# The opening of a hybrid decoder step: samples of x in one 128-row tile, the first x chunk in halves, first weights on another queue

## The chip, the cores and the metric

The kernel runs on one core of a Trainium2 chip. The metric is the device time of one execution in microseconds (us). Before the change, three runs gave a median of 1380.89 us (1379.9 to 1382.13). The engines are named as the profile names them: PE (TensorE; PEld is its weight load), DVE (VectorE), ACT (ScalarE), POOL (GpSimd) and SP (SyncE, which here only issues DMAs).

## The reference, cut to what matters

One layer of a decoder for 256 prompt tokens and 8 x 4 sample tokens, 288 rows of x with 2048 features: state-space heads and sliding-window attention side by side, a cross-attention to 256 memory tokens, a SwiGLU feed-forward, RMS norms before each. The change concerns only the first lines of it:

```
def rmsnorm(x, w):
    y = x * rsqrt(mean(x * x, axis=-1) + EPS)
    return y * w
h = rmsnorm(x, norm_mix)
proj = h @ w_in        # 2048 -> z, xbc, dt, q, k, v
```

The kernel multiplies x with `norm_mix` before the product and with the reciprocal root after it, so products can start before the mean of the squares is known.

## The kernel before, in words

All activations are kept transposed: features on the 128 partitions, the 288 rows of x (256 prompt, 32 sample) along the free axis. A product in full accuracy is three products of parts (`mm3`, L167 to L171): each operand is split into a rounded high part and the remainder, and the terms low x high, high x high and high x low are summed in PSUM. The three lines L169, L170 and L171 are nearly all of PE's work. Weights come by `wload` (L142): a DMA on SP's queue into a `raw` buffer (3 of them), a cast on ACT to `hi` (L159), a subtraction on DVE to `lo` (L79).

The opening (L339 to L362) runs over four chunks of 512 features of x. For a chunk, `load_x` (L273) brings three tiles by SP: 128 + 128 prompt rows and 32 sample rows, 512 features each. `split_x` (L280) transposes them in pieces of 128 features on PE (L118; three pieces for one k, four k in a chunk) into one PSUM tile for each k, ACT writes the high part times `norm_mix` (L85, tile `xa`), DVE the remainder (L82), and DVE copies the transposed x itself (L293). `square_x` (L296) sums squares on ACT. Into these steps go the products of the keys and values (256 columns of `w_in`, two weight tiles of two k in chunk 0) and those of the first queries (`q_chunk`, one 512 KB tile for a chunk, whose columns are permuted while they are cast). `NWARM` = 8 products on zeros stand twice as fillers, at L219 and L345; in plain f32 each call is two passes on PE.

The order of the instructions on each engine is fixed at build time by a planner: it takes the instructions that are ready in its own model of time, the earliest in the program first, unless `high_priority` moves a block ahead; the whole opening is moved ahead. `in_turn` (L120) keeps the marked instructions of an engine in program order among themselves. The planner also puts in the waits, by the regions of the tiles that instructions read and write. POOL's queue issues the loads of the small vectors at the start (L228 to L240), ACT's queue that of `norm_mix`. An `Exp` on an empty column at L212 makes ACT load its function table early.

Of the kernel before, what the change touches and what calls it, by code (L numbers as in the profile page):

```python
# [8 lines left out]
F32 = mybir.dt.float32  # L9
F32R = mybir.dt.float32r  # L10
I32 = mybir.dt.int32
AF = mybir.ActivationFunctionType
# [3 lines left out]
P = 128  # L16
D = 2048
KC = D // P
TP = 256
TS = 32  # L20
# [26 lines left out]
def tile_hymba_step(ctx: ExitStack, tc: tile.TileContext, I: dict, O: list, stop: int = 99):  # L47
# [4 lines left out]
    def tl(pool, shape, dt, tag):  # L52
        uid[0] += 1
        return pool.tile(shape, dt, name=f"{tag}_{uid[0]}", tag=tag)
# [27 lines left out]
        nc.vector.scalar_tensor_tensor(out=out, in0=in0, scalar=s, in1=in1, op0=op0, op1=op1)  # L82

    def act(out, in_, func, scale=1.0, bias=0.0, accum_out=None):
        nc.scalar.activation(out=out, in_=in_, func=func, scale=scale, bias=bias, accum_out=accum_out)  # L85

    def f32(ap):
        return ap.bitcast(F32)
# [26 lines left out]
    def transpose(out, in_):  # L115
        k = in_.shape[0]
        b = in_.base_partition() if callable(in_.base_partition) else in_.base_partition
        nc.tensor.transpose(out, in_, ident[b:b + k, 0:k])  # L118

    def in_turn(ins):  # L120
        tc.keep_in_program_order(ins)
# [17 lines left out]
            clock[0] = max(clock[0], pend[0][0])  # L139
            step(0)  # L140

    def wload(pieces, nk, nm, ahead=AHEAD, perm=False):  # L142
        raw = tl(p_raw, [P, 1024], F32, "raw")
        hi = tl(p_hi, [P, 1024], F32R, "hi")
        lo = tl(p_lo, [P, 1024], F32R, "lo")
        n = nk * nm
        rv, hv, lv = (t[:, :n].rearrange("p (k m) -> p k m", m=nm) for t in (raw, hi, lo))
        with tc.high_priority(offset=ahead):
            for sel, ap in pieces:
                nc.sync.dma_start(sel(rv), ap)  # L150
        with tc.high_priority(offset=min(ahead, SPLIT_AHEAD)):
            if perm:
                src = raw[:, :n].rearrange("p (k g m c) -> m p k g c", g=2, m=2, c=64)
                h_, l_ = (t[:, :n].rearrange("p (k m g c) -> m p k g c", g=2, m=2, c=64) for t in (hi, lo))
                parts = [(h_[m], l_[m], src[m]) for m in range(2)]
            else:
                parts = [(hi[:, :n], lo[:, :n], raw[:, :n])]
            for h_, l_, src in parts:
                nc.scalar.copy(h_, src)  # L159
# [120 lines left out]
    def split_x(cp, pcs):  # L280
        pss = []
        for k in range(4):
            kk = cp * 4 + k
            ps = psum()
            pss.append(ps)
# [5 lines left out]
        for k in range(4):  # L291
            st = tl(p_xb, [P, T], F32, "xb")
            nc.vector.tensor_copy(st, pss[k][:, :T])  # L293
            xst.append(st)

    def square_x(cp, pcs):  # L296
        for t3 in range(3):
            n = P if t3 < 2 else TS
            act(tm(n=n), pcs[t3][:n], AF.Square, accum_out=ssqx[:n, t3, cp:cp + 1])

    def x_rstd():
        rx = stat[:, 22:25]
# [22 lines left out]
    def tm(w=512, n=P, dt=F32):  # L325
        return tl(mxm, [P, 512], dt, "m")[:n, :w]
# [9 lines left out]
                 wq[:, k0:k0 + nk, O_Q + 512 * g + P * rp:O_Q + 512 * g + P * rp + P]) for g in range(2)], nk  # L336

    pkq = [acc() for _ in range(4)]
    xp_ = load_x(0)  # L339
    for cp in range(4):  # L340
        if cp == 0:
            kvw = [wload(wslice(w_in, 2 * i, 2, O_K, 256), 2, 256, 0) for i in range(2)]
            split_x(0, xp_)
            for _ in range(NWARM):
                nc.tensor.matmul(pkq[3][:, 0:P], wm, wm, start=True, stop=True)  # L345
            square_x(0, xp_)
        else:
            kvw = [wload(wslice(w_in, 4 * cp, 4, O_K, 256), 4, 256, 0)]
        qw = [wload(*q_chunk(0, 4 * cp), 256, ahead=0, perm=True)]
        if cp < 3:  # L350
            xp_ = load_x(cp + 1)
        if cp == 2:
            nc.sync.dma_start(cst[:, C_ONE:], I["cst"][:, C_ONE:])
        gemm_w(pkq[:2], kvw, 4 * cp, KC, xmix)
        if cp < 3:
            square_x(cp + 1, xp_)
            split_x(cp + 1, xp_)
            if cp == 2:
                x_rstd()
        else:  # L360
            x_rstd_rows()
        gemm_w(pkq[2:], qw, 4 * cp, KC, xmix)  # L362
# [1095 lines left out]
```

## Time and profile before

| | us |
|---|---|
| median of three runs | 1380.89 |
| profiled execution | 1382.05 |
| its span | 1380.3 |
| PE busy in the span | 1367.6 |
| DVE busy | 810.5 |
| ACT busy | 638.4 |
| POOL busy | 84.4 |

The span runs from the first to the last instruction of the profiled execution; the execution's own time has in addition what lies around it. PE's busy time counts pipelined matmuls, which overlap, so it says that something is always under way on PE, not that it runs at its peak. The chain of work goes back from the last instruction to what released it, step by step. The granted TensorE clock is at full speed through the whole span.

### The profile page before, as it was taken

The page shows a single profiled execution, that of the slowest core. Times are in us where ns is not written, and L with a number is a line of the kernel's source. Part 1 is how long each engine was busy: PE and PEld are TensorE (multiplying, and loading weights), DVE is VectorE, ACT ScalarE, POOL GpSimd, SP SyncE. Part 2 cuts the span into 40 slices and gives each one's busy share as a digit, 9 for nine tenths or more (in the row PEclk, how much of TensorE's full clock was granted, in tenths as well). Part 3 has the DMA queues.
Part 4 walks back from the last instruction along what each step waited for, and adds up shares of the span by engine and source line. Part 5 has one row for each costly group of instructions (what it writes and reads, how often), then busy time and mean ns, then how long its engine had stood idle before and what let it go on. Part 6 is the DMA issues. An engine that isn't in the chain of part 4 may idle for free.

```text
span 1380.3 us, 26140 instructions
## 1 busy us (share of the span) xinstructions
PE 1367.6 (99%) x10637; PEld 1334.1 (97%) x10637; DVE 810.5 (59%) x1444; ACT 638.4 (46%) x1042; POOL 84.4 (6%) x139
## 2 busy tenths in 40 slices
PE   9999999999999999999999999999999999999997
PEld 8999999999998999999999999999999999999997
DVE  6886798876565567545545444444544544545554
ACT  7456867644454556433333333333333433434332
POOL 2010100004210122000000000000000000000110
PEclk9999999999999999999999999999999999999999
DMA  9665476588558645555555555555555555555552
GB/s 255 187 195 141 127 229 199 145 246 222 168 168 272 207 149 169 168 168 166 164 164 165 168 163 163 165 167 171 165 168 168 167 169 165 164 158 166 167 169 92
DMA packets 251392, 241.17 MB, mean 175 GB/s; under 512 B 12778, under 2 KB 242576, under 8 KB 251272
## 3 DMA queue, kind: packets, MB, share of 16 engines
q1 hardware_dynamic: 248424, 234.79, 55.7%
q0 software_dynamic: 2816, 4.70, 1.4%
q8 instruction: 83, 1.36, 0.4%
q14 instruction: 37, 0.30, 0.1%
q10 hardware_dynamic: 32, 0.01, 0.0%
HBM read 227.59 MB, written 11.85 MB: 173 GB/s over the span
## 4 chain that ended last, share of the span: by engine, by line
PE 96%; DVE 2%; ACT 1%; issue 1%; DMA 0%; POOL 0%; DVEq 0%; ACTq 0%; POOLq 0%
PE mm L169 29%; PE mm L170 29%; PE mm L171 29%; PE ps L118 3%; DVE xa L82 1%; PE ps L823 0%; DVE lo L79 0%; PE ps L521 0%; DMA xT<-xspill 0%; PE ps L1162 0%; ACT hi L159 0%; PE ps L899 0%; PE ps L1197 0%; PE ps L912 0%; PE ps L1235 0%
## 5 line engine op out<-in xcount | busy, mean ns | idle before, releaser
L79 DVE TENSOR_TENSOR lo<-raw,hi 128x1024 fp32r<-128x1024 f32 (+1 forms) x413 | 478.1, 1160 | 449.4 <-ACT hi L159 444.4
L159 ACT CAST hi<-raw 128x1024 fp32r<-128x1024 f32 (+1 forms) x413 | 410.5, 997 | 542.1 <-PE mm L171 446.7
L169 PE MATMUL mm<-xa,lo 128*128 128x288 f32 x2016 | 599.8, 298 | 0.6 <-ACT xa L174 0.6
L170 PE MATMUL mm<-xa,hi 128*128 128x288 f32 x2016 | 597.0, 296 | 0.0
L171 PE MATMUL mm<-xa,hi 128*128 128x288 f32 x2016 | 590.3, 293 | 0.0
L169 PEld LDWEIGHTS mm<-xa,lo 128*128 128x128 f32 x2016 | 378.0, 187 | 4.8 <-issue 3.1
L171 PEld LDWEIGHTS mm<-xa,hi 128*128 128x128 f32 x2016 | 379.1, 188 | 1.0 <-issue 0.7
L170 PEld LDWEIGHTS mm<-xa,hi 128*128 128x128 f32 x2016 | 378.8, 188 | 0.9 <-issue 0.3
L169 PE MATMUL mm<-ls,lo 128*128 128x288 f32 x512 | 152.4, 298 | 0.0
L171 PE MATMUL mm<-ls,hi 128*128 128x288 f32 x512 | 151.6, 296 | 0.0
L170 PE MATMUL mm<-ls,hi 128*128 128x288 f32 x512 | 151.0, 295 | 0.0
L169 PE MATMUL mm<-xb,lo 128*128 128x288 f32 x448 | 132.2, 295 | 2.9 <-DVE xT L79 2.8
L170 PE MATMUL mm<-xb,hi 128*128 128x288 f32 x448 | 132.6, 296 | 0.0
L171 PE MATMUL mm<-xb,hi 128*128 128x288 f32 x448 | 131.9, 294 | 0.0
L79 POOL TENSOR_TENSOR ssum<-ssum,ls 128x288 f32<-128x288 f32 x43 | 47.5, 1104 | 881.4 <-ACT ls L85 880.5
L170 PEld LDWEIGHTS mm<-ls,hi 128*128 128x128 f32 x512 | 96.7, 189 | 0.1
L169 PEld LDWEIGHTS mm<-ls,lo 128*128 128x128 f32 x512 | 96.6, 189 | 0.1
L171 PEld LDWEIGHTS mm<-ls,hi 128*128 128x128 f32 x512 | 96.3, 188 | 0.0
L169 PEld LDWEIGHTS mm<-xb,lo 128*128 128x128 f32 x448 | 84.6, 189 | 3.6 <-DVE xT L79 3.4
L171 PEld LDWEIGHTS mm<-xb,hi 128*128 128x128 f32 x448 | 84.6, 189 | 0.2 <-DVE xb L79 0.2
L170 PEld LDWEIGHTS mm<-xb,hi 128*128 128x128 f32 x448 | 84.0, 188 | 0.1
L79 DVE TENSOR_TENSOR xT<-xT,mm 128x288 f32<-128x288 f32 x64 | 28.2, 448 | 42.3 <-PE mm L171 37.5
(301 smaller groups left out, 1126.4 us busy)
## 6 DMA issues: line engine op xcount, KB each, us to landing
raw<-in_w_gate_dram SPq DMA_DIRECT2D x88, 512.0 KB
raw<-in_w_up_dram SPq DMA_DIRECT2D x88, 512.0 KB
raw<-in_w_down_dram SPq DMA_DIRECT2D x80, 512.0 KB
raw<-in_w_in_dram SPq DMA_DIRECT2D x43, 512.0 KB
raw<-in_w_in_dram SPq DMA_DIRECT2D x34, 256.0 KB
raw<-in_w_out_dram SPq DMA_DIRECT2D x32, 256.0 KB
raw<-in_w_out_dram SPq DMA_DIRECT2D x16, 512.0 KB
ld<-in_state_ssm_dram SPq DMA_DIRECT2D x16, 256.0 KB
```

What stands on the lines that cost most here:

```text
L79: eng.tensor_tensor(out=out, in0=in0, in1=in1, op=op)
L82: nc.vector.scalar_tensor_tensor(out=out, in0=in0, scalar=s, in1=in1, op0=op0, op1=op1)
L118: nc.tensor.transpose(out, in_, ident[b:b + k, 0:k])
L159: nc.scalar.copy(h_, src)
L169: nc.tensor.matmul(ps, wl, xh, start=start, stop=False)
L170: nc.tensor.matmul(ps, wh, xh, start=False, stop=False)
L171: nc.tensor.matmul(ps, wh, xl, start=False, stop=stop)
```

## The change

- The 32 sample rows are no longer loaded as a tile of their own for each chunk. One tile `xsm` of 128 x 512 is cleared; its rows 0 to 31 get features 0 to 511 of the samples by ACT's queue, and, after the transposes of chunk 0, rows 32 to 127 get the other three chunks by POOL's queue. The sample piece of a k is a plain product of the 128-row tile with a slice of 32 columns of the identity, which selects the rows of the chunk.
- The two prompt tiles of chunk 0 are loaded in halves of 256 features, and chunk 0 is split in two steps of two k, with the products of the first weight tile between them in the program.
- The two weight tiles of the keys and values of chunk 0 are issued by ACT's queue.
- The transposes, the squares, the query casts and the second weight cast are kept in program order on their engines; the `Exp` moves behind the query casts of chunk 0, and the squares of chunk 0 behind it.

```diff
-    act(stat[:, 60:61], stat[:, 60:61], AF.Exp)
...
-    def load_x(cp):
-        pcs = [tl(p_ld, [P, 512], F32, "ld") for _ in range(3)]
-        for t3 in (2, 0, 1):
-            n = P if t3 < 2 else TS
-            nc.sync.dma_start(pcs[t3][:n], xps[t3][:, cp * 512:(cp + 1) * 512])
+    def load_x(cp, halves=1):
+        pcs = [tl(p_ld, [P, 512], F32, "ld") for _ in range(2)]
+        w = 512 // halves
+        for c0 in range(0, 512, w):
+            for t3 in range(2):
+                nc.sync.dma_start(pcs[t3][:, c0:c0 + w], xps[t3][:, cp * 512 + c0:cp * 512 + c0 + w])
         return pcs
...
-            for t3 in range(3):
-                n = P if t3 < 2 else TS
-                transpose(ps[:, t3 * P:t3 * P + n], pcs[t3][:n, k * P:(k + 1) * P])
+            for t3 in range(2):
+                in_turn(transpose(ps[:, t3 * P:t3 * P + P], pcs[t3][:, k * P:(k + 1) * P]))
+            in_turn(nc.tensor.matmul(ps[:, TP:T], xsm[:, k * P:(k + 1) * P], ident[:, TS * cp:TS * cp + TS],
+                                     start=True, stop=True))
...
-    xp_ = load_x(0)
+    xsm = tm()
+    nc.vector.memset(xsm, 0.0)
+    nc.scalar.dma_start(xsm[0:TS], xps[2][:, 0:512])
+    xp_ = load_x(0, 2)
     for cp in range(4):
         if cp == 0:
-            kvw = [wload(wslice(w_in, 2 * i, 2, O_K, 256), 2, 256, 0) for i in range(2)]
-            split_x(0, xp_)
+            kvw = [wload(wslice(w_in, 0, 2, O_K, 256), 2, 256, 0, queue=nc.scalar)]
+            split_x(0, xp_, (0, 1))
+            kvw.append(wload(wslice(w_in, 2, 2, O_K, 256), 2, 256, 0, queue=nc.scalar, turn=in_turn))
             for _ in range(NWARM):
                 nc.tensor.matmul(pkq[3][:, 0:P], wm, wm, start=True, stop=True)
-            square_x(0, xp_)
+            gemm_w(pkq[:2], kvw[:1], 0, KC, xmix)
+            split_x(0, xp_, (2, 3))
+            for c in range(1, 4):
+                nc.gpsimd.dma_start(xsm[TS * c:TS * c + TS], xps[2][:, 512 * c:512 * c + 512])
         else:
             kvw = [wload(wslice(w_in, 4 * cp, 4, O_K, 256), 4, 256, 0)]
-        qw = [wload(*q_chunk(0, 4 * cp), 256, ahead=0, perm=True)]
+        qw = [wload(*q_chunk(0, 4 * cp), 256, ahead=0, perm=True, turn=in_turn)]
+        if cp == 0:
+            in_turn(act(stat[:, 60:61], stat[:, 60:61], AF.Exp))
+            square_x(0, xp_)
...
-        gemm_w(pkq[:2], kvw, 4 * cp, KC, xmix)
+        gemm_w(pkq[:2], kvw[-1:], 4 * cp + (2 if cp == 0 else 0), KC, xmix)
```

## Rows read from the trace of the kernel before

**Rows 1.** The page's busy table and its chain by engine.

```profile
PE 1367.6 (99%) x10637; PEld 1334.1 (97%) x10637; DVE 810.5 (59%) x1444; ACT 638.4 (46%) x1042; POOL 84.4 (6%) x139
...
PE 96%; DVE 2%; ACT 1%; issue 1%; DMA 0%; POOL 0%; DVEq 0%; ACTq 0%; POOLq 0%
```

**Rows 2.** The chain of waits from 0 to 14 us: start, length, what.

```profile
8.96 1.31 PE mm L345 x10
10.28 0.13 PE mm L169
```

**Rows 3.** The timeline from 0 to 60 us: start, length, engine, line, what [idle before].

```profile
0.74 0.41 ACTq L214 DMA_DIRECT2D vec<-in_norm_mix_dram  x1
...
1.19 1.28 ACT L85 ACT_TABLE_LOAD   x1 [1.19 <-PEq L1446]
...
2.48 0.20 ACT L85 ACTIVATE stat<-stat 128x1 f32<-128x1 f32 x1
...
4.91 0.52 POOL L228 DMA_DIRECT2D vec<-in_conv_b_dram  x1
...
5.03 0.63 ACT L85 ACTIVATE m<-ld 128x512 f32<-128x512 f32 x1 [2.34 <-DMA ld<-in_x_prompt_dram]
...
6.13 0.63 ACT L85 ACTIVATE m<-ld 128x512 f32<-128x512 f32 x1 [0.38 <-DMA ld<-in_x_prompt_dram]
...
7.70 0.50 ACT L85 ACTIVATE xa<-ps,vT 128x288 fp32r<-128x288 f32 x1 [0.84 <-PE ps L118]
...
8.10 0.61 ACT L159 CAST hi<-raw 128x512 fp32r<-128x512 f32 x1
...
8.67 0.45 DVE L293 COPY xb<-ps 128x288 f32<-128x288 f32 x1
...
9.03 1.31 DVE L79 TENSOR_TENSOR lo<-raw,hi 128x512 fp32r<-128x512 f32 x2
...
10.03 0.38 PE L169 MATMUL mm<-xa,lo 128*128 128x288 f32 x1
...
14.32 1.04 ACT L159 CAST hi<-raw 128x1024 fp32r<-128x1024 f32 x1
...
15.39 1.23 DVE L79 TENSOR_TENSOR lo<-raw,hi 128x1024 fp32r<-128x1024 f32 x1
```

**Rows 4.** The chain of waits further on, its longer pieces to 86 us.

```profile
13.49 2.02 PE ps L118 x12
15.51 0.33 PE mm L169
...
85.86 0.23 PE mm L169
```

**Rows 5.** PE's weight loads in the timeline, about 13, 85 and 1366 us.

```profile
13.19 0.27 PEld L118 LDWEIGHTS ps<-cst,ld 128*128 128x128 f32 x2
13.63 0.38 PEld L118 LDWEIGHTS ps<-cst,ld 32*128 32x128 f32 x3 [0.17 <-issue]
...
85.46 0.30 PEld L480 LDWEIGHTS ps<-s,cst 128*128 128x128 f32 x2
85.68 0.19 PEld L169 LDWEIGHTS mm<-xa,lo 128*128 128x128 f32 x1
...
1366.15 0.47 PEld L118 LDWEIGHTS mm<-cst,xT 128*128 128x128 f32 x4
```

**Rows 6.** Busy time by window: engines, granted clock, DMA share, GB/s.

```profile
4.00:5.00 1.00, 1.00 (x6) 0.78 (x4) 0.00 (x0) 0.00 (x0) 1.00 (x3) 1.00 0.97 290
...
6.00:7.00 1.00, 1.00 (x7) 1.00 (x6) 0.00 (x0) 0.72 (x2) 0.40 (x2) 1.00 1.06 355
```

**Rows 7.** POOL's DMA issues: count, KB each, median us to landing.

```profile
out_dram<-s POOLq DMA_DIRECT2D x2, 64.0 KB, 3.2
...
hv<-in_dt_bias_dram POOLq DMA_DIRECT2D x1, 0.1 KB, 5.8
...
out_dram<-m POOLq DMA_DIRECT2D x2, 248.0 KB, 8.5
```

More of the change, by code (lines that the diff above doesn't have):

```diff
@@ L84, in act @@
     def act(out, in_, func, scale=1.0, bias=0.0, accum_out=None):
-        nc.scalar.activation(out=out, in_=in_, func=func, scale=scale, bias=bias, accum_out=accum_out)
+        return nc.scalar.activation(out=out, in_=in_, func=func, scale=scale, bias=bias, accum_out=accum_out)
     def f32(ap):
@@ L117, in transpose @@
         b = in_.base_partition() if callable(in_.base_partition) else in_.base_partition
-        nc.tensor.transpose(out, in_, ident[b:b + k, 0:k])
+        return nc.tensor.transpose(out, in_, ident[b:b + k, 0:k])
     def in_turn(ins):
@@ L140, in flush, with wload @@
             step(0)
-    def wload(pieces, nk, nm, ahead=AHEAD, perm=False):
+    def wload(pieces, nk, nm, ahead=AHEAD, perm=False, queue=nc.sync, turn=lambda i: i):
         raw = tl(p_raw, [P, 1024], F32, "raw")
@@ L149, in wload @@
             for sel, ap in pieces:
-                nc.sync.dma_start(sel(rv), ap)
+                queue.dma_start(sel(rv), ap)
         with tc.high_priority(offset=min(ahead, SPLIT_AHEAD)):
@@ L158, in wload @@
             for h_, l_, src in parts:
-                nc.scalar.copy(h_, src)
+                turn(nc.scalar.copy(h_, src))
                 tt(nc.vector, l_, src, f32(h_), ALU.subtract)
@@ L271, in tile_hymba_step, with split_x @@
     xps = [I["x_prompt"][0, 0:P], I["x_prompt"][0, P:2 * P], I["x_sample"].rearrange("b t d -> (b t) d")]
-    def load_x(cp):
-        pcs = [tl(p_ld, [P, 512], F32, "ld") for _ in range(3)]
-        for t3 in (2, 0, 1):
-            n = P if t3 < 2 else TS
-            nc.sync.dma_start(pcs[t3][:n], xps[t3][:, cp * 512:(cp + 1) * 512])
-        return pcs
-    def split_x(cp, pcs):
-        pss = []
-        for k in range(4):
+    def load_x(cp, halves=1):
[4 more added lines that the diff above has]
+                nc.sync.dma_start(pcs[t3][:, c0:c0 + w], xps[t3][:, cp * 512 + c0:cp * 512 + c0 + w])
+        return pcs
+    def split_x(cp, pcs, ks=range(4)):
+        pss = {}
+        for k in ks:
             kk = cp * 4 + k
             ps = psum()
-            pss.append(ps)
-            for t3 in range(3):
-                n = P if t3 < 2 else TS
-                transpose(ps[:, t3 * P:t3 * P + n], pcs[t3][:n, k * P:(k + 1) * P])
+            pss[k] = ps
+            for t3 in range(2):
+                in_turn(transpose(ps[:, t3 * P:t3 * P + P], pcs[t3][:, k * P:(k + 1) * P]))
+            in_turn(nc.tensor.matmul(ps[:, TP:T], xsm[:, k * P:(k + 1) * P], ident[:, TS * cp:TS * cp + TS],
+                                     start=True, stop=True))
             act(xh[kk], ps[:, :T], AF.Copy, scale=nwcol(V_MIX, kk))
             stt(xl[kk], ps[:, :T], nwcol(V_MIX, kk), f32(xh[kk]), ALU.mult, ALU.subtract)
-        for k in range(4):
+        for k in ks:
             st = tl(p_xb, [P, T], F32, "xb")
@@ L296, in square_x @@
     def square_x(cp, pcs):
-        for t3 in range(3):
-            n = P if t3 < 2 else TS
-            act(tm(n=n), pcs[t3][:n], AF.Square, accum_out=ssqx[:n, t3, cp:cp + 1])
+        for t3 in range(2):
+            in_turn(act(tm(), pcs[t3], AF.Square, accum_out=ssqx[:, t3, cp:cp + 1]))
+        in_turn(act(tm(n=TS), xsm[TS * cp:TS * cp + TS], AF.Square, accum_out=ssqx[:TS, 2, cp:cp + 1]))
     def x_rstd():
```

## The prediction, made before the changed kernel was run

> **What bounds the kernel now.** I read the busy table and the chain of the page first: TensorE (PE) is busy 99% of the span and makes up 96% of the chain that ends last [rows 1]. So after its first product PE is a belt without gaps: the end moves by the time at which the belt starts, by the PE work on it, and by gaps that the change tears into it. A faster engine beside it is worth nothing.
>
> Second view: the chain of the first 14 us [rows 2]. PE runs fillers on zeros (L219, L345) and transposes until the first product takes its place in the chain at 10.28; its own row starts at 10.03, and ten filler passes stand directly before it. From 10.28 to 13.49, where the next transposes stand, are 24 products, 0.134 us each [rows 2, 4]. The fillers show that PE waits for data here although no wait is listed. Third view: who makes the first product late [rows 3]. The two prompt tiles of x are there at 5.03 and 6.13 (the squares on ACT start on them), the transposes complete the first PSUM tile at 7.70 (ACT had waited 0.84 for it), then ACT scales (0.50) and casts the weights (0.61), DVE subtracts (2 x 0.65, with a copy of 0.45 pushed ahead), and the product comes 2.33 us after 7.70. Fourth: the transposes of the later chunks [rows 4, 5].
>
> **The change part by part.** The profiled execution took 1382.05, with a span of 1380.3; the sum below is a difference inside that span, and I put it on the median of the runs, 1380.89.
>
> *Opening.* Before, ahead of the end of the second x tile stood 64 KB of constants, 64 KB of samples and 512 KB of x on one queue: 640 KB by 6.13. After, 64 KB and the two first halves (256 KB) stand there, while ACT's queue (samples 64 KB, weights 512 KB) runs beside it. If ACT's queue gets as much as SP's, again 640 KB have moved and nothing is won; if ACT starts 0.9 us later (two issues of 0.4 us [rows 3]), some 450 KB, and at 290 to 355 GB/s [rows 6] the halves are there 0.6 earlier, at 5.5. The weights come sooner, since they no longer stand behind the second half of x. Only the two blocks of the first k must then be transposed (2 x 0.135, and two passes for the samples, 0.22, below), with 0.27 to the result: 6.3 against 7.70. From there 0.50 + 0.61 + 0.65 + 0.1: 8.2. The second halves follow some 0.9 us after the first, and their transposes (0.98) are done by 8.3; they fill time in which PE would wait. So the belt starts near 8.4 to 8.6 in the chain instead of 10.28. I take -1.6; from both sides -2.4 (weights cast before x is there) and -0.3 (no earlier half; only the filler passes between 10.03 and 10.28 go).
>
> *Sample transposes, chunks 1 to 3.* The rows of weight loads show the pattern for one k: two loads of 128 rows (0.27 together), 0.17 of idle "issue", one load of 32 rows (0.13) [rows 5]. A chunk costs 2.02, and the product behind it takes 0.33 in place of 0.13: 2.22; there are three on the belt [rows 4]. The new sample piece is a product of 128 rows: no change of height, but plain f32, which this trace runs in two passes (L480: one call, x2). They start 0.22 before the next load, 0.11 each; the product behind shows 0.23, so 0.10 for the way back [rows 4, 5]. A chunk is then 8 x 0.135 + 8 x 0.11 + 0.10 = 2.06, or 1.86 if the transposes go at 0.11 as near the end of the kernel; with the passes at the fillers' 0.131 it is 2.23 [rows 2, 5]. Gain per chunk 0.16 to 0.36, from no gain to 0.4: I take 0.25, in all -0.75 (0 to -1.2).
>
> *Samples by POOL.* Pieces 1 to 3 are written to rows 32 to 127 of the one tile whose 128 rows the chunk 0 pieces read; so they cannot be issued before the sample piece of k = 3, at about 8.3, and every sample piece of chunk 1 waits for all three. This wait is new. Issues on POOL take 0.5 each [rows 3], the third starts at 9.3. Chunk 0's key/value products end at 8.4 + 24 x 0.134 = 11.6; behind them on PE stand the transposes of chunk 1, which are held in order, so the third and all later ones queue behind a late sample piece, and ACT and DVE behind those. Before shows POOL transfers of 64 KB that land 3.2 us after issue: 12.5, 0.9 late, less 0.27 for the two prompt blocks that go ahead: +0.6. Bounds: 0 (landing within 2.6, or query products ordered into the gap) and 3.2 (5.8 us, the slowest small one in the opening) [rows 7]. I take 0.6, since size and kind match that row.
>
> *The Exp warm-up.* Before, its table load (1.28) and the Exp (0.20) run while ACT waits [rows 3]. Moved behind the query casts they stand where ACT has no pause. What waits for ACT next is the key/value weights of chunk 1: cast 14.32 to 15.36, subtracted by 16.62 [rows 3], used after 24 query products, 15.51 + 24 x 0.134 = 18.7; margin 2.1. ACT now squares later (two squares of 0.63 stood before 7.7), but starts on the critical work 1.3 earlier: level. With PE 1.6 ahead the margin is 0.5, and with the table load and the Exp in between it is 1.0 short. If the load already comes with the first copy on ACT, the Exp alone costs nothing. I take +0.3 (0 to 1.0), nearer to the second. The Trainium skill ("ScalarE: Activation LUTs", What ACT_TABLE_LOAD costs) adds about 1.38 us of drain to a switch of tables; here Exp follows its load at 2.48 without a pause, so the row decides. By the page this term could reach 2.4.
>
> *Hidden.* The memset of the sample tile comes before DVE has data; ACT's three DMA issues (1.2 us) lie ahead of its first data at 5.5; POOL is busy 6% of the span [rows 1], and without cover its issues would only push work that waits for later tiles. SP loses two weight issues, and its x loads wait less for buffers, since a chunk takes two tiles, not three: worth nothing while PE sets the pace.
>
> Sum: -1.6 - 0.75 + 0.6 + 0.3 = -1.45, so 1379.4. A measurement of this kernel tells about 0.2% (2.8 us) from no change; the sum is half of that.
>
> **Rivals.**
> A. Everything lands: opening -2.4, chunks -1.2, no new wait: -3.6, 1377.3. For it: POOL's wait is covered if query products stand ahead of chunk 1's transposes. Against: before, that order was transposes first [rows 4].
> B. The opening gives nothing, because the same bytes pass the same engines: -0.3 - 0.75, with no new wait as PE comes later: 1379.8. For it: 640 KB by 6.13 under equal shares. The Trainium skill says this outright ("DMA: Bandwidth & Descriptors", Issuing engines are not separate DMA queues): issuing from several engines saves only issue time, as all run on the same DMA engines. By that rule the weights on ACT's queue take from x what SP no longer has in front of it. No row of before has two large queues side by side.
> C. Slower: POOL's three pieces decide. The price is the wait at chunk 1, landing minus 11.9. With 8.5 us, the 248 KB row [rows 7], the third is there at 17.8: 5.9 us of gap on -2.05 of gains, +3.85, 1384.7. It eats the gain from a landing 4.7 us after issue and is worse by 0.2% from 7.4. For it: the small POOL loads of the opening needed 5.8 under full DMA load. Against: 64 KB took 3.2.
> D. The change doesn't do what it says on PE: two passes and the way back cost what the idle 0.17 and the 32-row load did, and the weights still set the first product: 0 to -0.3, 1380.7.
>
> **How the numbers follow.** Forecast 0.48 (own range 1378.0 to 1381.0), A 0.22, B 0.16, C 0.10, D 0.04. The range goes 0.7 below A, for an order of the instructions that I cannot see, and above to a POOL landing of 7.1 us (4.5 of wait on -2.05): 1376.6 to 1383.3. Faster by over 0.2% (below 1378.1): most of A and the low edge of the forecast, 0.26. Slower (above 1383.7): over half of C, and 0.06 for gaps I do not see: 0.12. Within: 0.62.
>
> **What would show it.** First product near 8.4 in the chain; no idle "issue" before sample pieces, and chunk transposes near 2.05; an ACT or DVE gap on PE near 17 to 18; a wait of a PE load for the sample tile near 12 to 13, its length the POOL landing. A start after 9.5, or a gap over 2 us there, makes the forecast wrong.

## The result, and the profile after

The changed kernel is slower. Six runs gave a median of 1387.88 us (1384.53 to 1388.96), the kernel before beside it 1380.64 (six runs, 1379.35 to 1382.29): a ratio of 1.0043 [1.0034, 1.0053]. The forecast was 1379.4 with a range up to 1383.3, so it is wrong in sign and outside its range. The profiled execution after is the fastest of the six (1384.53, span 1382.8); the difference of the two profiled executions is therefore smaller than that of the medians, and a second trace of the same kernel was taken later (below).

The busy table and the chain of the page after; the lines answer to [rows 1].

```profile
PE 1365.7 (99%) x10653; PEld 1334.7 (97%) x10653; DVE 811.8 (59%) x1445; ACT 638.5 (46%) x1042; POOL 85.9 (6%) x142
...
PE 94%; DVE 2%; DMA 1%; ACT 1%; issue 1%; POOL 0%; DVEq 0%; ACTq 0%; POOLq 0%
```

PE is busy 1.9 us less and the span is 2.5 longer: PE was made to stand. PE's share of the chain fell from 96% to 94%, and DMA, 0% before, is 1%. Who holds PE is in the waits of PE after (what waits, for whom: sum, times, longest):

```profile
PE ps L288 <- DMA m<-in_x_sample_dram: 3.4, 1, 3.4
```

Where they come from is in POOL's timeline after,

```profile
8.14 0.61 POOL L239 DMA_DIRECT2D hv<-in_d_skip_dram  x1
11.70 1.53 POOL L354 DMA_DIRECT2D m<-in_x_sample_dram  x3 [2.95 <-PE ps L288]
```

and in the list of DMA issues after (count, KB each, median us to landing):

```profile
m<-in_x_sample_dram POOLq DMA_DIRECT2D x3, 64.0 KB, 6.2
```

POOL is ready at 8.75, waits 2.95 us for PE's sample pieces of chunk 0 (L288), issues from 11.70 to 13.2, and a piece lands 6.2 us after its issue (the median of the three). PE's timeline after shows both ends of this (start, length, engine, line, what [idle before]; only the first products of each group are copied):

```profile
5.06 0.34 PE L118 MATMUL ps<-cst,ld 128*128 128x128 f32 x1
6.33 0.33 PE L118 MATMUL ps<-cst,ld 128*128 128x128 f32 x1 [0.93 <-DMA ld<-in_x_prompt_dram]
...
7.25 1.81 PE L350 MATMUL mm<-ld 128*128 128x128 f32 x14
8.82 0.38 PE L169 MATMUL mm<-xa,lo 128*128 128x288 f32 x1
...
10.49 0.38 PE L118 MATMUL ps<-cst,ld 128*128 128x128 f32 x2
10.71 0.31 PE L288 MATMUL ps<-cst,m 128*128 128x32 f32 x2
...
11.61 0.40 PE L169 MATMUL mm<-xa,lo 128*128 128x288 f32 x1 [0.20 <-ACT xa L85]
...
13.32 0.38 PE L118 MATMUL ps<-cst,ld 128*128 128x128 f32 x2
13.91 0.40 PE L169 MATMUL mm<-xa,lo 128*128 128x288 f32 x1 [0.21 <-DVE lo L79]
...
19.23 0.61 PE L288 MATMUL ps<-cst,m 128*128 128x32 f32 x2 [3.43 <-DMA m<-in_x_sample_dram]
...
21.89 0.59 PE L169 MATMUL mm<-xa,lo 128*128 128x288 f32 x1
...
25.63 0.30 PE L169 MATMUL mm<-xa,lo 128*128 128x288 f32 x1
...
28.42 0.38 PE L118 MATMUL ps<-cst,ld 128*128 128x128 f32 x2
...
29.96 0.38 PE L169 MATMUL mm<-xa,lo 128*128 128x288 f32 x1
...
36.39 0.38 PE L118 MATMUL ps<-cst,ld 128*128 128x128 f32 x2
...
57.07 2.15 PE L437 MATMUL ps<-xb,ld 128*32 128x288 f32 x32
```

Read it against the same view of before, of which these rows of the same stages go with [rows 3]:

```profile
13.32 2.19 PE L118 MATMUL ps<-cst,ld 128*128 128x128 f32 x12
...
22.05 2.08 PE L118 MATMUL ps<-cst,ld 128*128 128x128 f32 x11
...
30.55 2.19 PE L118 MATMUL ps<-cst,ld 128*128 128x128 f32 x12
...
51.71 2.15 PE L426 MATMUL ps<-xb,ld 128*32 128x288 f32 x32
```

The first product stands at 8.82 instead of 10.03 [rows 3], 1.2 earlier. Twelve products later the transposes of blocks 2 and 3 come at 10.49, now on the belt, and with ACT's 0.20 behind them they take it to 11.61. The first blocks of chunk 1 stand at 13.32, to the hundredth where the row of before stands in the timeline: the 1.2 us are gone. Then twelve query products slip in, and PE stands for 3.43 us until the third sample piece is there. What follows is in the windows after (us, busy us of PE, PEld, DVE, ACT and POOL with counts, the granted clock, DMA share, GB/s):

```profile
18.00:19.00 1.00, 0.00 (x0) 0.00 (x0) 0.00 (x0) 0.20 (x1) 0.00 (x0) 0.89 1.03 317
19.00:20.00 1.00, 0.77 (x4) 0.80 (x5) 0.00 (x0) 0.12 (x1) 0.00 (x0) 0.50 1.09 354
...
24.00:25.00 1.00, 1.00 (x6) 1.00 (x6) 0.98 (x4) 0.98 (x4) 0.00 (x0) 0.50 0.97 270
25.00:26.00 1.00, 1.00 (x7) 1.00 (x7) 1.00 (x3) 0.99 (x3) 0.00 (x0) 0.70 0.73 218
26.00:27.00 1.00, 1.00 (x10) 1.00 (x9) 0.66 (x2) 0.56 (x1) 0.00 (x0) 1.00 0.00 0
```

After PE had stood for some 3 us (from 15.8), the granted clock falls to 0.50, the level of 1.2 GHz in place of 2.4, and stays there until 25.6 although PE works again from 19.23. A window of 1 us then holds 6 matmuls, against 10 at full clock.

So the loss can be added up from the rows. Chunk 1 starts at 13.32 and chunk 2 at 28.42: 15.10 us. The same stretch without a wait takes 7.99, by PE's timeline of e14, a run below:

```profile
13.40 0.38 PE L118 MATMUL ps<-cst,ld 128*128 128x128 f32 x2
...
21.39 0.38 PE L118 MATMUL ps<-cst,ld 128*128 128x128 f32 x2
```

So 7.1 are lost. Of these 3.43 are the wait. The rest of the transposes takes 2.66 (19.23 to 21.89) against 1.33 at full clock, and the next 15 products 3.74 (21.89 to 25.63) against 15 x 0.134 = 2.01: 3.06 for the clock. 0.6 is left for 0.21 of DVE and small pieces. The fall is not a matter of this one trace: the mean granted clock listed for each run is 0.995 or 0.996 in all six runs of after and 0.994 or 0.995 in the four of after_again (below), and 0.997 to 0.999 in the 22 runs of before beside those four. Over a span of 1383 us the means differ by an estimated 2.6 and 4.0 us of full clock. From the belt's other end, at full clock, a chunk's transposes now take 29.96 - 28.42 = 1.54, where the chain had 2.02 and a slow product behind [rows 4].

To follow the belt past the opening I use one mark: the start of the 32 products on the transposed x, the first stage behind the opening (L426 before; `ps<-xb,ld` in the timeline), 51.71 in the trace of before. After it stands at 57.07: +5.4. The span is only 2.5 longer; what lies behind the mark is taken up below.

### The profile page after: what moved, and what is told of

Read it like the earlier page. It is cut to its first block, busy times and chain, and to the rows that moved or that the text cites. A ratio compares the mean times of both kernels' runs of the same rounds, so it can differ in the third digit from the quotient of the medians.

```text
span 1382.8 us, 26181 instructions
## 1 busy us (share of the span) xinstructions
PE 1365.7 (99%) x10653; PEld 1334.7 (97%) x10653; DVE 811.8 (59%) x1445; ACT 638.5 (46%) x1042; POOL 85.9 (6%) x142
## 4 chain that ended last, share of the span: by engine, by line
PE 94%; DVE 2%; DMA 1%; ACT 1%; issue 1%; POOL 0%; DVEq 0%; ACTq 0%; POOLq 0%
PE mm L169 29%; PE mm L171 29%; PE mm L170 29%; PE ps L118 3%; DVE xa L82 1%; PE ps L834 0%; DVE lo L79 0%; PE ps L532 0%; DMA m<-in_x_sample_dram 0%; PE ps L1173 0%; ACT hi L159 0%; DMA xT<-xspill 0%; PE ps L910 0%; PE ps L1208 0%; PE ps L923 0%
```

## The experiments

Each has one trace and several runs. "Mark" is the start of that stage minus 51.71; "wait" is PE's longest wait in the opening besides that for x. Medians are beside the kernel before on the same chip.

| run | median | before | ratio [95%] | mark | PE's wait in the opening |
|---|---|---|---|---|---|
| after | 1387.88 | 1380.64 | 1.0043 [1.0034, 1.0053] | +5.4 | samples 3.4 |
| after_again | 1388.05 | 1381.46 | 1.0052 [1.0039, 1.0065] | +6.6 | samples 3.1 |
| e1_two_tiles_pool | 1385.64 | 1381.53 | 1.0022 [1.0011, 1.0032] | +0.3 | samples 1.8 |
| e2_one_tile_sp | 1385.07 | 1381.53 | 1.0018 [1.0008, 1.0028] | -0.1 | DVE lo 0.8 |
| e3_fill_gap | 1388.59 | 1379.82 | 1.0055 [1.0038, 1.0072] | +5.1 | samples 1.4 (fillers ahead) |
| e4_before_tile | 1381.37 | 1381.53 | 0.9994 [0.9983, 1.0006] | -2.4 | none |
| e5_no_sample_tile | 1386.04 | 1379.82 | 1.0041 [1.0025, 1.0058] | +4.3 | DVE lo 0.6 |
| e6_two_tiles_sp | 1385.55 | 1381.53 | 1.0027 [1.0013, 1.0041] | +1.9 | DVE lo 1.4 |
| e7_free_squares | 1386.23 | 1379.82 | 1.0040 [1.0025, 1.0055] | +4.2 | DVE stat 1.4 |
| e9_split_first | 1385.72 | 1379.82 | 1.0038 [1.0024, 1.0053] | +3.0 | DVE stat 1.5 |
| e10_rows_last | 1384.30 | 1381.46 | 1.0022 [1.0011, 1.0034] | +2.5 | x 1.3, DVE s 1.2 |
| e11_pool_only | 1386.09 | 1381.46 | 1.0035 [1.0022, 1.0047] | +2.7 | samples 2.5 |
| e12_whole_rows | 1385.10 | 1381.46 | 1.0025 [1.0016, 1.0035] | +3.9 | DVE s 0.7 |
| e13_rstd_early | 1381.27 | 1380.56 | 1.0008 [0.9997, 1.0018] | -0.7 | none over 0.4 |
| e14_more_fill | 1381.44 | 1380.56 | 1.0009 [0.9997, 1.0022] | -0.6 | ACT xa 0.6 |
| e15_before_tile_rstd | 1379.93 | 1380.56 | 0.9989 [0.9979, 0.9999] | -2.1 | DVE lo 0.1 |

The order of the medians is nearly that of the marks; single executions of one kernel lie up to 9 us apart (e6, 1381.35 to 1390.33), and one trace shows one of them. Much of that comes behind the mark: from there to the end the trace of after is 2.9 us shorter than that of before, that of e1 3.4 longer. One reason lies in a stage that no version touches. Near 320 us PE waits 2.3 to 3.2 us for DVE in all seventeen traces; in PE's waits of before it is

```profile
PE mm L169 <- DVE xT L79: 2.8, 1, 2.8
```

Behind it the granted clock falls to 0.50 for 3 to 7 us in thirteen of the traces and stays at 1.00 in four (before, after, e3, e13). So a mark of -0.7 need not show in a median.

**1. Is it the pieces?** Theory: the late pieces make PE wait. Rival: something else in the opening.

e2: the three pieces on SP's queue, still into the one tile.

```diff
-                nc.gpsimd.dma_start(xsm[TS * c:TS * c + TS], xps[2][:, 512 * c:512 * c + 512])
+                nc.sync.dma_start(xsm[TS * c:TS * c + TS], xps[2][:, 512 * c:512 * c + 512])
```

> The changed kernel, one tile as it is, pieces 1 to 3 issued by SP instead of POOL at the same place of the program: they still wait for chunk 0's sample pieces (PE at 11.1). Theory T1 (order, not the queue): issue at 11.5 to 12.5, landing 3 us or more later at 15 to 16, a wait of 0 to 0.5 behind the 12 query products that end at 15.8; but SP's queue stands until 11.1, so the next weights come later: 1379 to 1383. Rival R (POOL's queue is what is slow): the same landing as that, and a gain of all the loss, 1379 to 1381. If the wait stays near 3 us, neither the queue nor its issuing engine matters, only the load on the DMA engines.

The wait for the samples is gone from the list, and the mark falls from +5.4 to -0.1. SP issues from 11.38 to 12.65, as late as POOL did, and PE reads the pieces at 16.10, behind sixteen query products and without a wait: the third is under way for at most 3.9 us, against 6.4 for POOL's (12.74 to 19.10). The median is 3.5 over before, where the changed kernel's was 7.2: half of the loss hangs on who brings the pieces. What the other 3.5 are, this trace, with its mark of -0.1, does not show.

e1: a second cleared tile for chunks 1 to 3, still issued by POOL.

```diff
...
-    xsm = tm()
+    xsm, xs1 = tm(), tm()
+    nc.vector.memset(xs1, 0.0)
...
-                nc.gpsimd.dma_start(xsm[TS * c:TS * c + TS], xps[2][:, 512 * c:512 * c + 512])
+                nc.gpsimd.dma_start(xs1[TS * c:TS * c + TS], xps[2][:, 512 * c:512 * c + 512])
```

> The changed kernel, with pieces 1 to 3 in a second tile but still issued by POOL: the write no longer waits for the reads of chunk 0. Theory T1 (the late issue at 11.7 is the cause): issue at 8.8 to 9.8, right behind the small vectors, landing near 14 to 15, a wait of PE of about 1 us, no fall of the clock, 1379 to 1381. Rival R (POOL's transfers need 6 us or more under full DMA load whenever they are issued): landing after 16, a wait of over 2.5 us, and the planner has put no query products into it: 1382 or more.

POOL issues from 8.99 instead of 11.70, since nothing has to be read first; the landing still takes 5.3 us, and PE still waits 1.8. So both halves of the delay count: that the issue waits for PE, and that the piece is long on its way. The median, 4.1 over before, is more than the mark of +0.3 explains: in this execution the granted clock falls to 0.50 once more from 164 to 171 us, behind no wait of PE's.

e6: the second tile, and the pieces issued by SP ahead of x chunk 1.

> The changed kernel, with pieces 1 to 3 of the samples in a second 128-row tile, issued by SP ahead of the x tiles of chunk 1, so that they wait for nothing. Theory T (the loss is PE's 3.4 us wait for the third POOL piece and the 2.9 us that the halved clock after it costs): no wait at the first sample piece of chunk 1, clock at full speed throughout, transposes of a chunk near 1.55, and 1378 to 1380, at or below the kernel before. Rival S (the new order of the opening costs it: halves, weights on ACT's queue, the Exp): still above 1383 although no sample piece is late.

No wait for samples, yet 1.0027: a new wait, PE for DVE's lo, 1.4 us at 21.43. ACT's timeline of e6 shows whose it is:

```profile
12.83 0.90 ACT L85 ACTIVATE xa<-ps,vT 128x288 fp32r<-128x288 f32 x2 [4.03 <-PE ps L291]
...
17.95 0.63 ACT L85 ACTIVATE m<-m 32x512 f32<-32x512 f32 x1
...
19.08 1.03 ACT L159 CAST hi<-raw 128x1024 fp32r<-128x1024 f32 x1
```

From 14.76 ACT does six squares in program order, those of two chunks, ahead of chunk 1's splits and the key/value cast at 19.08, which before stood at 14.32 [rows 3]. Before that ACT had been idle for 4.03, because blocks 2 and 3 came late from PE. `in_turn` on the squares makes this order.

e3: the wait left as it is, with 24 products on the identity put ahead of the first sample piece of chunk 1.

```diff
+            if kk == 4:
+                for _ in range(24):
+                    in_turn(nc.tensor.matmul(ps[:, 384:512], ident, ident, start=True, stop=True))
             in_turn(nc.tensor.matmul(ps[:, TP:T], xsm[:, k * P:(k + 1) * P], ident[:, TS * cp:TS * cp + TS],
...
```

> The changed kernel with 24 products of the identity with itself (two passes each, into unused columns of the PSUM tile) on PE between the second prompt block and the first sample piece of chunk 1; they fill the wait, and the 12 query products that stood in it come behind. Theory C (half of the loss is the clock that falls while PE stands): granted clock 1.00 through 15 to 26 us, the sample piece at 19 to 20 as before, chunk 2's transposes start at 26.5 to 27.5 in place of 28.4, and 1385 to 1387 against 1387.9, although PE has 1.6 us of products less inside the wait. Rival W (only the wait counts): without those 12 products in it the kernel is 1.6 slower, 1389 or more.

PE's timeline of e3:

```profile
13.30 0.38 PE L118 MATMUL ps<-cst,ld 128*128 128x128 f32 x2
13.52 5.52 PE L290 MATMUL ps<-cst 128*128 128x128 f32 x48
20.39 0.38 PE L291 MATMUL ps<-cst,m 128*128 128x32 f32 x2 [1.35 <-DMA m<-in_x_sample_dram]
...
28.27 0.38 PE L118 MATMUL ps<-cst,ld 128*128 128x128 f32 x2
```

A row of its windows, as those above:

```profile
22.00:24.00 2.00, 2.00 (x16) 2.00 (x16) 1.62 (x5) 1.96 (x5) 0.62 (x3) 1.00 1.05 263
```

The granted clock is 1.00 in every row of the opening: here PE, kept at work to 19.04, kept its clock through the 1.35 us that it still stood. But the fillers stand ahead of the twelve query products, and the pieces landed at 20.4. Chunk 1 to chunk 2 takes 14.97, against 7.99 without a wait: the 6.98 lost are nearly the 6.87 from 13.52, where the fillers start, to 20.39. Two kernels lose the same 7 us there, one by wait and clock, one by wait alone. So this run does not part the clock from the wait by its time, as it was meant to (chunk 2 at 26.5 to 27.5 was expected, 28.27 came): what it saves of the clock's 3.06 goes again by the query products that now stand behind (1.6) and by pieces that land 1.2 later than in after. The time that the data needs can't be filled away.

**2. Is that part enough by itself?** e11 is the kernel before with the one sample tile and POOL's three issues, and nothing else of the change.

```diff
...
+            for c in range(1, 4):
+                nc.gpsimd.dma_start(xsm[TS * c:TS * c + TS], xps[2][:, 512 * c:512 * c + 512])
...
```

> The kernel before with one part of the change alone: one 128-row tile of the samples, its last three pieces issued by GpSimd behind the transposes of chunk 0. Weights, x chunks, Exp and squares as before. Theory (the wait for the pieces and the clock behind it are enough): pieces issued from about 9.3 to 10.8 us, landing 5.5 to 6.3 us after, so that TensorE waits at chunk 1 from about 14 to 17 us, 2.5 to 3.5 us; the granted clock falls to 0.5 for some microseconds behind it; the mark at 297 to 300, the median 3 to 6 us over the kernel before. Rival (the opening's order is what made the pieces late, and the tile alone is harmless): the wait under 1 us, clock 1.00, the median at or under the kernel before.

The theory's numbers came: issues from 9.01 to 11.0, landing 5.4, a wait of 2.5, the clock at 0.50 behind it, 4.6 us over before. A row of PE's waits in e11:

```profile
PE ps L289 <- DMA m<-in_x_sample_dram: 2.5, 1, 2.5
```

Its windows:

```profile
18.00:20.00 2.00, 2.00 (x11) 2.00 (x10) 1.95 (x4) 2.00 (x7) 0.49 (x3) 0.50 0.64 210
20.00:22.00 2.00, 2.00 (x12) 2.00 (x12) 1.98 (x6) 1.98 (x6) 0.00 (x0) 0.65 0.60 136
```

Here the first product stands at 9.68 and there is no new order of the opening, so the rival (only the new order makes the pieces late) falls.

e4 is the kernel before with the sample tiles issued by SP, two tiles, nothing waited for.

```diff
...
+        if cp == 1:
+            for c in range(1, 4):
+                nc.sync.dma_start(xs1[TS * c:TS * c + TS], xps[2][:, 512 * c:512 * c + 512])
...
```

> The kernel before, with the 128-row sample tiles alone (two tiles, all pieces by SP early; x in whole tiles, weights on SP, Exp at the start). What the sample piece by identity slices is worth by itself: the transposes of a chunk 1.54 in place of 2.02, and 0.13 in place of 0.33 for the next product, so 0.6 to 0.7 for each of three chunks: 1378.5 to 1379, 2 us under the kernel before. By the prediction's estimate of 0.25 a chunk: 1379.9.

The mark moves to -2.4, the best of all runs: the tile's transposes gain on PE, as the prediction had it, and more (chunk 1 to chunk 3 takes 15.96, 12.79 to 28.75, against 17.23 before). The median is the same as before within its interval.

**3. What does the new opening do without the tile?** e5 is the changed kernel with the samples loaded as before, a 32-row tile for each chunk on SP.

> The changed kernel without the sample tile: samples as tiles of 32 rows by SP, transposed as before; halves, weights on ACT's queue, Exp and squares in order as changed. Theory P (all of the loss is POOL's pieces): no wait, the opening gives something, 1380 to 1382. Theory P+A (the squares of chunk 0 and 1, which now stand in order behind the query casts, make ACT late for the key and value weights of chunk 1, as in the kernel with SP's pieces: there PE waited 1.4 for the subtraction): again a wait of 1 to 2 us for a subtraction near 20 us, transposes of a chunk 2.0, and 1384 to 1387.

1.0041 without any wait for samples: this kernel loses too. Its longest waits are small (DVE lo 0.6, x 0.4), but from 10 to 20 us PE ran only 57 matmuls, in before 73. PE was slow there, not idle: twelve filler passes and the first twelve products take 5.55 us (8.24 to 13.79), where the pace of after, 0.112 and 0.134 each, makes 2.95. These 2.6 are most of the 3.35 by which chunk 1 starts later than before (16.67). The clock record of this trace starts only at 13.7 us, and the rows ahead of it show 1.00 for want of a record; more on that with after_again. So this run does not show that the new order loses by itself.

e7: e6 with squares that need not keep their order. e9: e7 with blocks 2 and 3 transposed ahead of the first products.

```diff
-            in_turn(act(tm(), pcs[t3], AF.Square, accum_out=ssqx[:, t3, cp:cp + 1]))
+            act(tm(), pcs[t3], AF.Square, accum_out=ssqx[:, t3, cp:cp + 1])
...
-            gemm_w(pkq[:2], kvw[:1], 0, KC, xmix)
             split_x(0, xp_, (2, 3))
+            gemm_w(pkq[:2], kvw[:1], 0, KC, xmix)
```

> The kernel with two tiles and SP's pieces, with the squares no longer held in program order on ACT: the planner puts those of chunk 0 into ACT's idle time before its second half of x. Theory A: the wait for the subtraction of chunk 1 goes (1.4 to under 0.3), the kernel gets 1.5 to 3 faster than 1385.6: 1382 to 1384, and the clock stays up in more runs. Rival: the wait stays because the weights land late (raw tile), no change.

> As the last, and the second split of chunk 0 stands ahead of the first products in the program. Theory O (the opening won nothing because the transposes of k = 2, 3 went onto the belt and ACT and DVE stood still meanwhile): first product near 8.8, all 24 key and value products in one row without a gap, done 0.9 earlier than 13.5, and the kernel ends under the one before: 1379 to 1381. Rival: the second halves of x hold up the first products (start after 9.5), 1381 to 1383.

In both the wait for DVE's lo is gone, so the squares' order was its cause. In e9 24 key/value products run in a row from 9.33, and chunk 3 starts at 28.81, 1.7 ahead of before (30.55). Both are slow all the same, by a wait further on. DVE's timeline of e9:

```profile
36.08 0.15 DVE L79 TENSOR_TENSOR stat<-stat 128x3 f32<-128x3 f32 x1
36.15 0.68 DVE L79 TENSOR_TENSOR lo<-raw,hi 128x512 fp32r<-128x512 f32 x1
36.75 0.15 DVE L82 SCALAR_TENSOR_TENSOR stat<-stat 128x3 f32<-128x3 f32 x1
```

PE's timeline of e9, the row that waits:

```profile
40.81 1.01 PE L315 MATMUL ps<-cst,stat 128*128 128x128 f32 x6 [1.48 <-DVE stat L82]
```

A window of e9 behind it:

```profile
43.00:44.00 1.00, 1.00 (x6) 0.88 (x5) 0.41 (x2) 0.00 (x0) 0.00 (x0) 0.50 1.14 337
```

The last tiny operations of `x_rstd()` are dealt out between subtractions of 0.68, one each; in before they run in a row from 27.91, but for the last. PE's row products (L315) wait 1.48, and this short gap too is followed by 7 us of half clock (42.3 to 49). Half of that is lost: it costs more than itself.

**4. Mending that.** e10 is e9 with `x_rstd()` ahead of the last split and the row products behind the last query products. e12: the same with x chunk 0 whole.

```diff
-            split_x(cp + 1, xp_)
             if cp == 2:
                 x_rstd()
-        else:
-            x_rstd_rows()
+            split_x(cp + 1, xp_)
         gemm_w(pkq[2:], qw, 4 * cp, KC, xmix)
+        if cp == 3:
+            x_rstd_rows()
```

> The opening of the changed kernel with its three waits taken out: the samples' pieces in a tile of their own, issued by SyncE ahead of x chunk 1; squares free to be moved; transposes of blocks 2 and 3 ahead of the first products (all as in the run with the transposes first), and now x_rstd() ahead of the last split and x_rstd_rows() behind the last 12 query products. Theory (gaps of TensorE and the clock after them made the change slow, nothing else in it costs): no wait over 0.7 us on TensorE between 6 and 60 us, granted clock 1.00 in every row from 10 to 60 us, the mark near 294 us (the cast that stands at 294.43 before) at 291 to 292.5, the median 1.5 to 3 us under the kernel before of the same chip. Rival (weights issued by ScalarE, or the halves, cost by themselves): the mark at 294 or later, the median 2 us or more over the kernel before, with a clock of 0.996 or less in the runs though no wait stands in the opening.

> The mended version once more with x chunk 0 whole instead of in halves: all four transposes of chunk 0 as soon as it lands, the first weights in two pieces issued by ScalarE, two sample tiles by SyncE, free squares, x_rstd_rows() behind the last query products. Theory (the halves win little): first product within 0.5 us of the mended version with halves, the mark within 1 us of it, the median within 1.5 us of it. Rival (the halves bring the first product forward): first product and mark 1 to 2 us later than with halves.

Both missed. The row products so late hold up DVE, which empties the accumulators with them: e10 waits 1.2 for DVE at 45.32 (e12 0.7), with a clock of 0.50 behind. And e10's x came late in this execution. Its first product stands at 11.63, e12's at 13.06. Windows of e10:

```profile
8.00:9.00 1.00, 1.00 (x8) 1.00 (x7) 0.83 (x2) 0.62 (x2) 0.89 (x2) 0.60 1.13 269
9.00:10.00 1.00, 1.00 (x7) 1.00 (x7) 0.57 (x2) 1.00 (x3) 0.00 (x0) 0.50 0.93 233
```

PE's timeline of e10, the fillers:

```profile
7.60 2.81 PE L354 MATMUL mm<-ld 128*128 128x128 f32 x14
```

ACT's timeline of e12, the cast of the second weight tile:

```profile
8.63 0.62 ACT L159 CAST hi<-raw 128x512 fp32r<-128x512 f32 x1 [2.10 <-DMA raw<-in_w_in_dram]
```

Fourteen filler passes stand ahead of the first product and take 2.81 in e10, at a clock of 0.50 from 8.2 on, where after had 1.81. In e12 the second weight tile on ACT's queue came at 8.6 and x on SP's queue at 7.29: neither is early. Its fourteen passes take 3.33, and its clock record starts at 13.9, behind its first product.

after_again is the changed kernel as it stands, for a second trace.

> The changed kernel as it stands, on the chip of these runs, for a second trace. Theory: the wait for the third sample piece again 3 to 4 us, granted clock 0.5 for 5 us or more behind it, the mark at 299 to 301, the median 6 to 9 us over the kernel before. Rival (the wait in the first trace was a chance of that execution): the wait under 1.5 us and the clock 1.00 in the opening, yet the median the same 7 us over.

PE's timeline of this second trace:

```profile
6.38 0.47 PE L118 MATMUL ps<-cst,ld 128*128 128x128 f32 x1 [0.84 <-DMA ld<-in_x_prompt_dram]
...
8.10 2.56 PE L350 MATMUL mm<-ld 128*128 128x128 f32 x14
...
10.42 0.38 PE L169 MATMUL mm<-xa,lo 128*128 128x288 f32 x1
...
20.48 0.61 PE L288 MATMUL ps<-cst,m 128*128 128x32 f32 x2 [3.10 <-DMA m<-in_x_sample_dram]
```

The wait for the samples is there again. The first product stands at 10.42, later than before, not 1.2 earlier: transposes take 0.47 in place of 0.33, fillers 2.56 in place of 1.81. With the same order of PE's work up to it, the first product stands at 8.27 to 8.82 in after, e1, e2 and e3, and at 10.13 to 10.60 here, in e6 and in e7: the gain is there in some executions and not in others, and in which of them is luck as far as is known.

The pace says what differs. One k of transposes takes 0.75 here (7.07 to 7.82), the very time that it takes behind the wait at a recorded clock of 0.50 (20.90 to 21.65), against 0.39 in after. The clock record of this trace starts at 9.7 us; the 1.00 that the rows show ahead of it is no record. In after, e1, e2 and e3 it starts at 4.1 to 5.4, in e6 and e7 at 10.5 and 9.7. So PE went at the lower level until then, and the first product is early where the clock rose early.

e13 puts the row products back and keeps the early `x_rstd()`, so that only the wait for the first x piece is left. e14 adds two fillers to the first group against that one. e15 is e4 with the early `x_rstd()`.

```diff
-    for _ in range(NWARM):
+    for _ in range(NWARM + 2):
         nc.tensor.matmul(pw[:, 0:P], wm, wm, start=True, stop=True)
```

> As the run with x_rstd_rows() behind the last products, but x_rstd_rows() back in its place; x_rstd() stays ahead of the last split. Theory (gaps and the clock behind them): no wait of TensorE over 0.7 us from 7 to 60 us; only that for the first x piece remains (0.6 to 1.7 us at 5.3 us), and where it is over 1 us the clock stands at 0.5 for some 4 us behind it. The mark at 291 to 294, the median 1 to 2 us under the kernel before, with runs spread over 4 us by that wait. Rival (ScalarE's weight issues or the halves cost by themselves): median 2.5 to 4 us over the kernel before, the loss seen in no wait.

> As the run with x_rstd() early, with two more filler matmuls in the first group (10 for 8), which reach to 5.8 us, so that the wait for the first x piece is 0 to 0.9 us. Theory: clock 1.00 in all rows to 60 us, first product at 9 to 9.6 us, the mark at 290.5 to 292, the median 1.5 to 3 us under the kernel before and more runs with a granted clock of 0.997 or above than in the version with 8. Rival: median 2.5 us or more over the kernel before all the same.

> The kernel before with two sample tiles issued by SyncE (the part of the change that gained) and x_rstd() ahead of the last split; opening as before. Theory: as the run with the tiles alone, mark at 292.5 to 293, median 0.5 to 2 us under the kernel before. Rival (chance of one chip, that run's 0.9994): same as the kernel before within 0.3 us.

With the gaps gone the loss is gone: 1.0008 and 1.0009, both with an interval that holds 1, and no record of a granted clock below 1.00 up to 60 us. So weights issued by ScalarE, the halves and the new order do not cost by themselves what e2 to e12 lost. But neither is a gain, and there I expected 1 to 3 us: e13's and e14's medians lie 1.3 and 1.5 over e15's on the same chip. In e13 the fillers are slow again (x14, 2.83), and chunk 1 starts at 14.33; in e14 they aren't (2.03), the first product stands at 9.48, chunk 1 at 13.40, but PE waits 0.6 at 36.08 for ACT. e14 was also to have more runs at a mean clock of 0.997 or above than e13: it has nine of twelve, e13 all twelve, and its three slowest (1384.84 to 1385.47) are the three with the lowest clock (0.993 to 0.995). e15, with the old opening, has its first product at 9.35.

e15 is faster than before by 0.1 to 2.9 us (0.9989 [0.9979, 0.9999]), the only version whose interval lies below 1, and only just. It has the tile's transposes with the pieces early, which the change contained, and the early `x_rstd()`, which it did not; e4, without the latter, is level (0.9994). So the gain of the tile by itself is shown in PE's timeline, in the medians it is not.

## Why the prediction was wrong

**The failed step is "Samples by POOL".** It gave the wait +0.6 us, with 3.2 as its bound; measured are 3.43 and 3.10. The mechanism was the right one: POOL can't overwrite rows 32 to 127 until the sample pieces of chunk 0 are read, and all pieces of chunk 1 wait for all three. Three of its numbers were off.
- When POOL can issue: forecast 8.3 to 9.3, measured 11.70 to 13.2. I had the transposes of blocks 2 and 3 fill PE's idle time ahead of the first product. They stood behind twelve products, as the program has them (`gemm_w` before `split_x(0, xp_, (2, 3))`). A release that hangs on PE's order is as late as that order makes it.
- How long a piece takes: 3.2 by a row at 52 us, measured 6.2 (5.4 in e11, 5.3 in e1). That row has the size but not the kind: it is of two stores to DRAM, and the pieces are loads. The loads of POOL in the same trace had needed 5.8 for a small one in the opening [rows 7] and 5.0 for 144 KB near 315 us (`xT<-xspill`). Full DMA engines alone don't tell them apart: the DMA share is 0.74 to 1.05 where the stores were under way and 0.96 to 1.25 where the pieces were. Why POOL's loads take so long is not shown; the same pieces issued by SP were faster (e2). The Trainium skill ("DMA: Bandwidth & Descriptors", Anatomy of one DMA — SWDGE (gpsimd) path) fits such a transfer by 2.0 us and 436 KB a us, which gives an estimate of 2.2; no run here in the opening came near it, so the measurement decides.
- What hides it: I had 24 products ahead of chunk 1 and none behind. There, twelve query products did slip in (13.91 to 15.8), else PE would have stood 5 us (3.43 and their 1.6).

**Missing altogether: the clock.** No term and no rival had it. Behind the wait PE runs at 0.50 of its clock for some 6 us, 3.06 us lost, nearly as much as the wait. The rows that I read could not show it: in the opening of before PE never stands, and behind its one long stand, the 2.8 us near 320, that trace stays at 1.00. But it is a price that a gap in the sum can bring, and with it the range would have reached past 1383.3.

**The opening.** Forecast -1.6, bounds -2.4 to -0.3; by the start of chunk 1 it is 0 (13.32 and 13.32), in the second trace +1.6 (14.94). The first halves of x were there at 6.33, where I had 5.5, and no earlier than all of the chunk before (6.13); the first PSUM tile was complete at 7.06, where I had 6.3. The weights were early, as forecast (cast at 5.11), and by the first trace the operands of the first product were ready at 7.56 (ACT's step on `xa`, 7.06 to 7.56, was the last). What failed then is what comes after: fillers of 1.57 to 2.3 us stand ahead of the first product in PE's order, and the 1.1 us of transposes that I placed in idle time went onto the belt. In the second trace the late rise of the clock comes on top. Rival B gave the other half of the truth, that nothing is won in transfers: by 6.13 640 KB had moved before; by 6.33 after it is 64 of constants and 256 of x on SP's queue, 64 of samples and 256 of weights (cast at 5.11) on ACT's, at least 640 KB again. By the page that I named with that rival ("DMA: Bandwidth & Descriptors", Issuing engines are not separate DMA queues, of the Trainium skill) it had to be so, and the trace agrees.

**Sample transposes.** Right in kind, too small: -0.25 each forecast, with 0.4 as bound. In PE's timeline chunk 2 to chunk 3 takes 7.97 us after (28.42 to 36.39) and 8.50 before (22.05 to 30.55), and chunk 1 to chunk 2 7.99 in e14, where nothing waits, against 8.73 before: -0.5 and -0.7. Before does the first block of chunk 2 already at 21.68, within the earlier stretch, so over both it is -0.6 for each. One k takes 0.39 (four in 1.54): I had two passes of 0.11 each, by the passes on 128 columns; on 32 columns both together start 0.14 before the next load (10.71 to 10.85).

**Exp.** Forecast +0.3; it cost nothing that shows. The table load came with ACT's first cast at 3.04 and ran while ACT waited. ACT's timeline after:

```profile
3.04 1.28 ACT L159 ACT_TABLE_LOAD   x1 [3.04 <-DMA vec<-in_norm_mix_dram]
...
12.88 0.20 ACT L85 ACTIVATE stat<-stat 128x1 f32<-128x1 f32 x1
```

The wait of 0.3 to 1.0 that I expected near 17 to 18 exists, 1.35 in e6, but by the squares that `in_turn` holds in order. In the changed kernel the wait for the samples covers it.

**The rivals.** C was the case: POOL's pieces decide, slower. Its formula (landing minus 11.9) gives 7.3 and 8.6 us for the landings at 19.2 and 20.5, where PE's waits end in the two traces; wait and clock together were 6.5 in the first, so its size is about right, for partly other reasons. It had a chance of 0.10, "against: 64 KB took 3.2", by the same row that misled the sum.

Added up for the first trace, from the marks: opening 0, chunk 1 to chunk 2 15.10 against 8.73, +6.4; chunk 2 to 3 -0.5; chunk 3 to the mark 20.68 against 21.16, -0.5: +5.4. For the second: +1.6, +5.9, -0.5, -0.5: +6.6. The medians differ by 7.2 and 6.6, the spans of the two traces from that of before by 2.5 and 8.0; the rest lies behind the mark and is not traced to the change.

## What to carry to other kernels

A buffer that is loaded again in a hurry inherits its readers' order: ask when the last reader runs on its engine, not when it could, and price the load by a transfer in the same stretch, under the same DMA load, not by one of equal size elsewhere. Where TensorE is a belt without gaps, a gap costs itself and can cost as much again or more in the clock behind it (0 to 3.4 us in these traces), so a step that can tear one needs more in return than its own length. A row that prices a transfer must match it in kind, load or store, and not only in size. Taking one wait away shows the next: four versions here each removed the wait named by the trace and met another of 1.2 to 1.5 us, and the level ones (e4, e13 to e15) have none over 0.6.

## What the runs showed of the hardware

- Granted clock after PE stood: 3.4 us of standing were followed by 7 us at 0.50 (after), 2.5 by 3.4 (e11), 1.48 by 7 (e9), 1.34 by 3 (e10). In e1 1.8 were followed by none in the opening, nor were 1.35 in e3 and in e6; the record of e1 falls later, to 0.93 over 150 to 200 us, behind no gap that its waits name. The wait of 2.3 to 3.2 near 320 us was followed by a fall in thirteen traces and by none in four. So a gap is not always followed, and its length doesn't set the cost.
- The clock record of a trace begins with a rise to 1.00, between 4.1 and 13.9 us; ahead of it the rows show 1.00 without a record. So the full clock that the text on before gives to the whole span holds from 7.1 us to 1375; PE is done then, and the clock falls to 0.50. The pace tells the level: fourteen filler passes took 1.81 in after, e3 and e9, whose records begin at 4.8 to 5.4, and 2.56 to 3.33 in after_again, e6, e7, e12 and e13, whose records begin at 9.7 to 13.9. With the old opening the record begins at 4.3 to 7.1 (before, e4, e11, e15), with the new one at 9.7 or later in six traces of thirteen. Whether the new opening makes the rise late, and so costs e13 what it lacks against e15, is not shown.
- Not tried: the pieces on ACT's queue, and a version of e15 with its remaining 0.4 us of wait for x filled. What is left between e15 and e13, 1.3 us of the new opening, is not taken apart by these runs.
